# A plain chunk moved to the auxiliary PSUM banks, a later norm product and a reordered weight split in a four-FFN decoder trunk

## The chip, the cores and the metric

One core of a Trainium2 chip runs the whole program in one launch. The metric is the device time of that core in microseconds (us); the time of a kernel is the median of its runs. The engines are named as in the profile: PE (matmul), DVE (vector), ACT (scalar), POOL (GpSimd), and SP, which issues the weight loads.

## What is computed

A decoder trunk over 512 tokens of width 1024, in float32. It has four SwiGLU FFNs (width 2816), with a pooling mixer between the first two and a latent attention between the last two:

```python
def rmsnorm(x, g):
    y = xf * lax.rsqrt(jnp.mean(xf * xf, axis=-1, keepdims=True) + RMS_EPS)
    return (y * g.astype(jnp.float32)).astype(x.dtype)

def swiglu(u, wg, wu, wd):
    return (jax.nn.silu(u @ wg) * (u @ wu)) @ wd
...
    for l in range(DEPTH):
        h = h + 0.5 * swiglu(rmsnorm(h, ffn_pre_norm[l]), ffn_pre_wg[l], ffn_pre_wu[l], ffn_pre_wd[l])
...
        h = h + 0.5 * swiglu(rmsnorm(h, ffn_post_norm[l]), ffn_post_wg[l], ffn_post_wu[l], ffn_post_wd[l])
```

## The kernel before, in words

Activations lie transposed: eight channels of 128 features by 512 tokens (`h[c]`). Float32 operands are split into a rounded high part and a low remainder, and each product takes three matmuls (`mm3`, L116 to L118). A weight tile of 128x1024 is loaded by SP into `wraw`, rounded by ACT (`whi`) and subtracted by DVE (`wlo`); this pair is the split (`load_w` L145, L146; `split_into` L188, L189).

The norm of an FFN is applied late. The matmuls run on `gain*h`, and the per-token factor `r` is multiplied in afterwards. `on_all` (L290) turns `r` into a tile `rb` of 128x512: DVE writes two diagonal tiles (L294, L303), PE multiplies them by ones (L301, L305, "the norm product" here), and ACT copies the result out of PSUM (L307).

PSUM has two pools here. `mm_tile()` hands out six banks in turn, `aux_tile()` two banks in turn. A bank handed out again may be written only when the readers of its last tile are done.

An FFN (`ffn`, L448) makes 22 chunks of 128 hidden features.

- Chunks 0 to 3 are plain: for each of the eight channels a gate and an up product of 512 columns. Chunks 0 and 1 run together in four mm banks, chunk 2 in two more (`m` = 0 gate, 1 up, L570 to L578), chunk 3 in two more (L586 to L589). The norm product is called inside chunk 2. `gated` (L527) then makes the hidden values: DVE multiplies the gate by `rb` (L530), ACT takes the silu (L516), DVE multiplies by `rb` again (L517) and by the up product (L533, which is the last reader of the up bank), and ACT and DVE split the result into `mh`, `ml` (L523, L524).
- Chunks 4 to 21 are the groups (L597). Gate and up weights and two halves of the tokens form 2x2 blocks, and Winograd's seven products take the place of eight. Each product P1 to P7 is 12 matmuls of 256 columns. A group accumulates in three mm tiles, x, y1 and y2. P1, P6, P7 and P4 add to x one after the other, and between them ACT copies x out (`copy_of`, L462: `c1` after P1, `c16` after P6, `c167` after P7). P6 has to wait for the copy `c1`, P7 for the copy `c16`. The operands `t3` of P7 are made by `prepare_t3` in place of half of four `gh` tiles.
- The group's weights come from `group_weights` (L191): two loads, then four splits and four POOL adds (L201). The last split (L213, L214) needs the last add.
- Between the products stand the down products (`down`, L539), 512 columns wide, in aux banks, each output channel `d` in a bank of its own. In group 4 the order on PE is P1, P2, early (d = 0 with chunks 0 and 1, then d = 1 with chunks 0 and 1), P6, P5, middle (d = 0 and 1 with chunk 2), P7. Group 5 goes on with P1, P2 and early (chunk 3).

PE's order is that of the code (`manual_schedule`). On DVE, ACT, POOL and SP a scheduler at build time sets the order; `queued_behind(steps)` tells it that what follows may not be issued ahead of the steps named. In the third FFN `rb` comes from the shared key/value stage ahead of it, so it has no norm product inside chunk 2.

Of the kernel before, what the change touches and what calls it, by code (L numbers as in the profile page):

```python
# [19 lines left out]
ND = D // P  # L20
# [22 lines left out]
def down_steps(g):  # L43


    i, base = g % PART, g - g % PART - PART
    most, end, whole = range(base, base + PART - 1), [base + PART - 1], range(base, base + PART)
    if i == 0 and base == 0:
        return ([(d, most[:2], True, False) for d in range(2)], [(d, most[2:], False, False) for d in range(2)], [])
    if i == 0:  # L50
        return [], [], [(d, most, True, False) for d in range(2)]
    early = [(d, end, False, True) for d in range(2)] if i == 1 else []
    return early, [], [(d, whole, True, True) for d in (2 * i, 2 * i + 1)]
# [15 lines left out]
def trunk_kernel(  # L69
# [23 lines left out]
    nc = tc.nc  # L93
# [11 lines left out]
    def f(ap):  # L105
        return ap.bitcast(F32)

    def mm_tile():
        return psum.tile([P, T], F32, tag="mm", name="mm")

    def aux_tile():
        return psaux.tile([P, T], F32, tag="aux", name="aux")

    def mm3(out, w, x, start, stop, **kw):

        nc.tensor.matmul(out, w[0], x[0], start=start, stop=False, **kw)  # L116
        nc.tensor.matmul(out, w[0], x[1], start=False, stop=False, **kw)  # L117
        nc.tensor.matmul(out, w[1], x[0], start=False, stop=stop, **kw)  # L118
# [61 lines left out]
    def split_w(raw, pool, tag):  # L180
        n = raw.shape[-1]
        hi = pool.tile([P, n], F32R, tag=f"{tag}hi", name=f"{tag}hi")
        lo = pool.tile([P, n], F32R, tag=f"{tag}lo", name=f"{tag}lo")
        return hi, lo

    def split_into(tiles, raw, s):
        hi, lo = tiles
        nc.scalar.copy(hi[:, s], raw[:, s])  # L188
        nc.vector.tensor_tensor(out=lo[:, s], in0=raw[:, s], in1=f(hi[:, s]), op=ALU.subtract)  # L189

    def group_weights(idx, g, wb):  # L191

        ra, rb = (wraw_sb.tile([P, UNIT], F32, tag="wraw", name="wraw") for _ in range(2))
        nc.sync.dma_start(ra, wgu[idx, g - 2, 0])
        nc.sync.dma_start(rb, wgu[idx, g - 2, 1])
        q0, q1, whole = slice(0, 512), slice(512, UNIT), slice(0, UNIT)

        def add(out, x, y):  # L200
            nc.gpsimd.tensor_tensor(out=out, in0=x, in1=y, op=ALU.add)  # L201

        a = split_w(ra, wsplit_sb, "w")
        split_into(a, ra, whole)
        a22 = split_w(rb[:, q0], room.wf, "f")
        split_into(a22, rb[:, q0], q0)
        add(rb[:, q0], rb[:, q0], rb[:, q1])
        add(rb[:, q1], rb[:, q1], ra[:, q0])
        s13 = split_w(rb, wsplit_sb, "w")
        split_into(s13, rb, whole)  # L210
        add(ra[:, q0], rb[:, q0], ra[:, q0])
        add(ra[:, q1], ra[:, q0], ra[:, q1])
        s24 = split_w(ra, wb, "w")  # L213
        split_into(s24, ra, whole)  # L214
        a, a22, s13, s24 = part(a, 8, P), part(a22, 4, P), part(s13, 8, P), part(s24, 8, P)

        def of(w, at):
            return lambda k: [x[:, at + k] for x in w]

        return dict(a11=of(a, 0), a12=of(a, 4), a22=of(a22, 0), s1=of(s13, 0), s3=of(s13, 4), s2=of(s24, 0), s4=of(s24, 4))  # L220
# [4 lines left out]
               before=lambda i, u=u: nc.sync.dma_start(h[2 * u + i], xT[:, 2 * u + i]))  # L225
# [156 lines left out]
    def part(w, *shape):  # L382

        names = "abcd"[:len(shape)]
        spec = f"p ({' '.join(names)}) -> p {' '.join(names)}"
        return [x.rearrange(spec, **dict(zip(names, shape))) for x in w]

    def queued_behind(steps):

        stack = ExitStack()  # L390
        for step in steps:
            stack.enter_context(tc.issue_after(step))
        return stack
# [54 lines left out]
    def ffn(idx, norm, on_h, first=None, last=None):  # L448
        with tc.tile_pool(name="mid", bufs=1) as midp, tc.tile_pool(name="wb", bufs=2) as wb, \
                tc.manual_schedule(engines={mybir.EngineType.PE}):  # L450
            weights, acc, act, mids = {}, {}, {}, {}

            def product(g, to, w, x, start=True):
                if start:
# [4 lines left out]

            def copy_of(g, name):  # L460
                t = act[g][name] = room.act.tile([P, HT], F32, tag=name, name=name)
                nc.scalar.copy(t, acc[g]["x"])  # L462
                return t

            def p1(g):
                product(g, "x", "a11", "b11")
                copy_of(g, "c1")

            def p2(g):
                product(g, "y2", "a12", "b21")  # L470
                y = acc[g]["y2"]
                nc.vector.tensor_tensor(out=y, in0=act[g].pop("c1"), in1=y, op=ALU.add)

            def gate_half(g, i, y):
                if i == 0:
                    act[g]["g"] = room.act.tile([P, T], F32, tag="g", name="gate", bufs=3)
                s = slice(i * HT, (i + 1) * HT)
                nc.vector.tensor_tensor(out=act[g]["g"][:, s], in0=y, in1=rb[:, s], op=ALU.mult)

            def p6(g):  # L480
                product(g, "x", "s2", "t2", start=False)
                copy_of(g, "c16")

            def p5(g):
                product(g, "y1", "s1", "t1")

            def p7(g):
                product(g, "x", "s3", "t3", start=False)
                copy_of(g, "c167")

            def up_half(g):

                t = act[g]["c167"]
                nc.vector.tensor_tensor(out=t, in0=t, in1=acc[g]["y1"], op=ALU.add)

            def p4(g):

                product(g, "x", "a22", "t4", start=False)
# [28 lines left out]
            def gated(g, gate, up):  # L527

                t = room.act.tile([P, T], F32, tag="g", name="gate", bufs=3)
                nc.vector.tensor_tensor(out=t, in0=gate, in1=rb, op=ALU.mult)  # L530
                silu(t)
                m = room.act.tile([P, T], F32, tag="m", name="m", bufs=3)
                nc.vector.scalar_tensor_tensor(out=m, in0=up, scalar=-1.0, in1=t, op0=ALU.mult, op1=ALU.mult)  # L533
                split_mid(g, m)

            units, o_of = {}, {}
            whole = slice(0, T)
# [19 lines left out]
            ps = [mm_tile() for _ in range(4)]  # L557
# [12 lines left out]
            for m in range(2):  # L570
                o = mm_tile()
                for c in range(ND):
                    mm3(o, [x[:, (c + 4 * m) % ND] for x in ws[m]], norm.gh[c], c == 0, c == ND - 1)
                    if m == 1 and c == 0:
                        rb = norm.spread(r, steps)
                        for j in range(2):
                            gated(j, ps[2 * j], ps[2 * j + 1])
                ps.append(o)  # L578
# [4 lines left out]

            with queued_behind(steps):
                weights[N_FIRST] = group_weights(idx, N_FIRST, wb)
            ps = [mm_tile() for _ in range(2)]  # L586
            for c in range(ND):
                for m in range(2):
                    mm3(ps[m], [x[:, (c + 4 * m) % ND] for x in ws[m]], norm.gh[c], c == 0, c == ND - 1)  # L589
# [6 lines left out]
            before = None  # L596
            for g in range(N_FIRST, NF):  # L597
                early, middle, late = down_steps(g)
                if g > N_FIRST:
                    weights[g] = group_weights(idx, g, wb)  # L600
                acc[g], act[g] = {}, {}
                p1(g)
                p2(g)
                gate_half(g, 0, acc[g].pop("y2"))
                for step in early:
                    down(*step, tile_of=aux_tile)
                if before is not None:
                    p4(before)
                p6(g)
                p5(g)  # L610
                for step in middle:
                    down(*step, tile_of=aux_tile)
                if g == NF - 1:
                    p7(g)
                    up_half(g)
                    p3(before)
                    p4(g)
                    p3(g)
                else:
                    if before is not None:  # L620
                        p3(before)
                    p7(g)
                    up_half(g)
                before = g
                for step in late:
                    down(*step, tile_of=aux_tile)
# [15 lines left out]
    nc.sync.dma_start(rope_sb, rope)  # L642
    nxt = Norm(G_MIX)
    ffn(0, norm, nxt.add, first=first_w)

    norm, nxt = nxt, Norm(G_POST)
# [60 lines left out]
    norm, nxt = nxt, Norm(G_PRE + ND)  # L707
    Quarters(nxt, inline=False)
    ffn(1, norm, nxt.add)


# [64 lines left out]
    with tc.tile_pool(name="att", bufs=2) as ap_, tc.tile_pool(name="att1", bufs=1) as a1:  # L776
# [190 lines left out]
        with tc.manual_schedule(engines={engines.PE}):  # L967
            ps = {0: weights(0, qk, nope_first=True)}
# [173 lines left out]
```

## Time and profile before

| | us |
|---|---|
| median of two runs | 1725.56 |
| the two runs | 1724.69, 1726.42 |
| the profiled execution, its own time | 1728.71 |
| its span, first to last instruction | 1726.9 |
| PE busy in the span | 1706.3 (99%) |
| DVE busy | 1302.8 (75%) |
| ACT busy | 850.9 (49%) |
| POOL busy | 570.0 (33%) |

A busy PE is not a PE at full speed: at half clock it is busy too. The mean granted clock of the execution is 0.995 of full speed.

### The profile page before, as it was taken

To read this page: it belongs to the slowest core of one execution; us is meant where nothing else is said; L and a number is where in the kernel's file an instruction comes from. 1 tells how busy PE (TensorE), PEld (TensorE's weight loads), DVE (VectorE), ACT (ScalarE), POOL (GpSimd) and SP (SyncE) were. 2 spreads that over 40 slices of the span, in tenths; PEclk is the share of its full clock that TensorE was granted. 3 is DMA by queue.
4 is the path that set the end of the run, shared out by engine and by line. 5 is a ranking of instruction groups with operands and counts; after the bars stand their busy time and mean duration, and the time that the engine had idled before them with its cause. 6 is when DMAs were issued, how large, how long until landed. Compare 5 with 4: busy or idle time off the path is not lost. (4 is left out here: it accounts for less than half of the span.)

```text
span 1726.9 us, 27436 instructions
## 1 busy us (share of the span) xinstructions
PE 1706.3 (99%) x10816; PEld 1543.4 (89%) x10816; DVE 1302.8 (75%) x2086; ACT 850.9 (49%) x1391; POOL 570.0 (33%) x388
## 2 busy tenths in 40 slices
PE   8999999999999999999999999999999999999998
PEld 6899999998899999888999999888888889999997
DVE  8877777789777777897777777787765787777775
ACT  6544444464444444454444444586655544444443
POOL 2433344133333344113334432422221234334421
PEclk9999999999999999999999999999999999999999
DMA  6233333322333322332333333332231232333331
GB/s 208 86 99 110 110 91 95 121 87 62 110 99 110 109 91 95 106 95 86 111 111 92 94 108 104 94 90 56 61 86 62 72 100 86 111 110 98 95 102 50
DMA packets 49585, 166.77 MB, mean 97 GB/s; under 512 B 6320, under 2 KB 6320, under 8 KB 49456
## 3 DMA queue, kind: packets, MB, share of 16 engines
q1 hardware_dynamic: 49312, 164.98, 31.1%
q8 instruction: 85, 1.39, 0.3%
q14 instruction: 44, 0.36, 0.1%
q10 hardware_dynamic: 144, 0.04, 0.0%
HBM read 158.44 MB, written 2.10 MB: 93 GB/s over the span
## 5 line engine op out<-in xcount | busy, mean ns | idle before, releaser
L201 POOL TENSOR_TENSOR wraw<-wraw 128x512 f32<-128x512 f32 x288 | 438.9, 1525 | 749.2 <-DVE flo L189 703.5
L116 PE MATMUL mm<-gh_hi,whi 128*128 128x256 f32 (+1 forms) x1424 | 435.2, 306 | 6.9 <-ACT c L462 6.9
L118 PE MATMUL mm<-gh_hi,wlo 128*128 128x256 f32 (+1 forms) x1424 | 435.1, 306 | 1.1 <-DVE wlo L146 1.1
L117 PE MATMUL mm<-gh_lo,whi 128*128 128x256 f32 (+1 forms) x1424 | 434.7, 305 | 0.5 <-DVE gh_lo L328 0.5
L188 ACT CAST whi<-wraw 128x1024 fp32r<-128x1024 f32 x216 | 226.9, 1053 | 207.7 <-POOL wraw L201 184.4
L116 PEld LDWEIGHTS mm<-gh_hi,whi 128*128 128x128 f32 x1424 | 274.6, 193 | 21.6 <-ACT c L462 8.6
L117 PEld LDWEIGHTS mm<-gh_lo,whi 128*128 128x128 f32 x1424 | 274.5, 193 | 14.3 <-DVE gh_lo L328 0.9
L118 PEld LDWEIGHTS mm<-gh_hi,wlo 128*128 128x128 f32 x1424 | 274.4, 193 | 13.4 <-DVE wlo L146 2.7
L189 DVE TENSOR_TENSOR wlo<-wraw,whi 128x1024 fp32r<-128x1024 f32 x216 | 271.3, 1257 | 3.1 <-ACT whi L188 3.0
L116 PE MATMUL aux<-mh,whi 128*128 128x512 f32 x576 | 225.3, 391 | 0.0
L117 PE MATMUL aux<-ml,whi 128*128 128x512 f32 x576 | 225.2, 391 | 0.0
L118 PE MATMUL aux<-mh,wlo 128*128 128x512 f32 x576 | 224.1, 389 | 0.0
L146 DVE TENSOR_TENSOR wlo<-wraw,whi 128x1024 fp32r<-128x1024 f32 (+1 forms) x158 | 184.8, 1170 | 31.0 <-ACT whi L145 30.6
L145 ACT CAST whi<-wraw 128x1024 fp32r<-128x1024 f32 (+2 forms) x188 | 162.3, 878 | 86.4 <-PE mm L117 46.7
L504 DVE TENSOR_TENSOR mm<-c,mm 128x256 f32<-128x256 f32 x72 | 30.9, 429 | 197.9 <-PE mm L118 197.9
L116 PE MATMUL mm<-t_hi,whi 128*128 128x256 f32 (+1 forms) x592 | 169.5, 286 | 0.6 <-ACT c L462 0.6
L118 PE MATMUL mm<-t_hi,wlo 128*128 128x256 f32 (+1 forms) x592 | 169.3, 286 | 0.0
L117 PE MATMUL mm<-t_lo,whi 128*128 128x256 f32 (+1 forms) x592 | 169.2, 286 | 0.0
L345 POOL TENSOR_TENSOR sq_acc<-sq_acc,sq 128x512 f32<-128x512 f32 (+1 forms) x47 | 72.5, 1543 | 203.1 <-ACT sq L341 193.4
L517 DVE TENSOR_TENSOR gate<-gate,rb 128x512 f32<-128x512 f32 x88 | 133.6, 1523 | 2.8 <-ACT gate L516 2.8
L462 ACT COPY c<-mm 128x256 f32<-128x256 f32 x216 | 79.8, 370 | 103.9 <-PE mm L118 103.9
L118 PEld LDWEIGHTS aux<-mh,wlo 128*128 128x128 f32 x576 | 108.2, 188 | 23.2
(209 smaller groups left out, 3328.2 us busy)
## 6 DMA issues: line engine op xcount, KB each, us to landing
wraw<-in_wgu SPq DMA_DIRECT2D x160, 512.0 KB, 3.7
wraw<-in_wd SPq DMA_DIRECT2D x88, 512.0 KB, 3.6
wraw<-in_wo SPq DMA_DIRECT2D x16, 512.0 KB, 3.8
wraw<-in_wfirst SPq DMA_DIRECT2D x12, 512.0 KB, 3.6
wraw<-in_wheads SPq DMA_DIRECT2D x8, 512.0 KB, 3.5
h<-in_xT SPq DMA_DIRECT2D x8, 256.0 KB, 5.4
wraw<-in_wfirst SPq DMA_DIRECT2D x8, 256.0 KB, 5.3
qr<-yh SPq DMA_DIRECT2D x32, 64.0 KB, 2.1
```

The costliest lines, as they stand in the source:

```text
L116: nc.tensor.matmul(out, w[0], x[0], start=start, stop=False, **kw)
L117: nc.tensor.matmul(out, w[0], x[1], start=False, stop=False, **kw)
L118: nc.tensor.matmul(out, w[1], x[0], start=False, stop=stop, **kw)
L145: nc.scalar.copy(hi[:, s], raw[:, s]).ins,
L146: lo_engines[i % len(lo_engines)].tensor_tensor(out=lo[:, s], in0=raw[:, s], in1=f(hi[:, s]), op=ALU.subtract).ins]
L188: nc.scalar.copy(hi[:, s], raw[:, s])
L189: nc.vector.tensor_tensor(out=lo[:, s], in0=raw[:, s], in1=f(hi[:, s]), op=ALU.subtract)
L201: nc.gpsimd.tensor_tensor(out=out, in0=x, in1=y, op=ALU.add)
L345: nc.gpsimd.tensor_tensor(out=self.acc[:, ts], in0=self.acc[:, ts], in1=self.sq[:, ts], op=ALU.add)
L462: nc.scalar.copy(t, acc[g]["x"])
L504: nc.vector.tensor_tensor(out=y, in0=act[g]["c16"], in1=y, op=ALU.add)
L517: nc.vector.tensor_tensor(out=gate, in0=gate, in1=rb, op=ALU.mult)
```

## The change

Three edits, all in `ffn` and the functions it calls.

1. Chunk 3's gate and up products go to the two aux banks in place of two mm banks.
2. The call that makes `rb` (the norm product and what follows it) stands in chunk 2 behind channel 4 in place of channel 0, so the two matmuls come four channels (12 matmuls) later.
3. From group 5 on, the group's last split is queued behind the copy `c16` of the group before.

```diff
-    def group_weights(idx, g, wb):
+    def group_weights(idx, g, wb, last_behind=()):
...
         s24 = split_w(ra, wb, "w")
-        split_into(s24, ra, whole)
+        with queued_behind(last_behind):
+            split_into(s24, ra, whole)
...
             def copy_of(g, name):
                 t = act[g][name] = room.act.tile([P, HT], F32, tag=name, name=name)
-                nc.scalar.copy(t, acc[g]["x"])
-                return t
+                copied[g, name] = nc.scalar.copy(t, acc[g]["x"]).ins
...
                     mm3(o, [x[:, (c + 4 * m) % ND] for x in ws[m]], norm.gh[c], c == 0, c == ND - 1)
-                    if m == 1 and c == 0:
+                    if m == 1 and c == ND // 2:
                         rb = norm.spread(r, steps)
...
-            ps = [mm_tile() for _ in range(2)]
+
+            ps = [aux_tile() for _ in range(2)]
...
                 if g > N_FIRST:
-                    weights[g] = group_weights(idx, g, wb)
+                    weights[g] = group_weights(idx, g, wb, [copied[before, "c16"]])
```

The lines of the changed kernel are one to three further down. Three places show what moves; all are taken from the first FFN, and the numbers behind the names are those of the buffers.

PE in group 4, at the end of P2 (`mm_688` is y2) and the early down products: `aux_704` is d = 0 and `aux_711` is d = 1. A name in brackets is the engine whose semaphore the matmul waits for. Before:

```order
L117 MATMUL mm_688<-gh7_lo_259,whi_573 128x256
L118 MATMUL mm_688<-gh7_hi_258,wlo_574 128x256
L116 MATMUL aux_704<-mh0_506,whi_564 128x512 [waits PE_49,Activation_49]
L117 MATMUL aux_704<-ml0_507,whi_564 128x512 [waits DVE_49]
L118 MATMUL aux_704<-mh0_506,wlo_565 128x512
L116 MATMUL aux_704<-mh1_516,whi_564 128x512 [waits Activation_49]
L117 MATMUL aux_704<-ml1_517,whi_564 128x512 [waits DVE_49]
L118 MATMUL aux_704<-mh1_516,wlo_565 128x512
L116 MATMUL aux_711<-mh0_506,whi_564 128x512
L117 MATMUL aux_711<-ml0_507,whi_564 128x512
```

The same place on PE in the changed kernel:

```order
L117 MATMUL mm_688<-gh7_lo_259,whi_573 128x256
L118 MATMUL mm_688<-gh7_hi_258,wlo_574 128x256
L116 MATMUL aux_704<-mh0_518,whi_564 128x512 [waits DVE_49,Activation_49]
L117 MATMUL aux_704<-ml0_519,whi_564 128x512
L118 MATMUL aux_704<-mh0_518,wlo_565 128x512
L116 MATMUL aux_704<-mh1_528,whi_564 128x512 [waits Activation_49]
L117 MATMUL aux_704<-ml1_529,whi_564 128x512
L118 MATMUL aux_704<-mh1_528,wlo_565 128x512
L116 MATMUL aux_711<-mh0_518,whi_564 128x512 [waits DVE_49]
L117 MATMUL aux_711<-ml0_519,whi_564 128x512
```

The order of the matmuls is the same, but the first one of d = 0 and the first one of d = 1 now wait for DVE. The two aux tiles handed out last were chunk 3's gate (`aux_593`) and up (`aux_594`), so d = 0 takes the bank of the gate and d = 1 that of the up product.

DVE around those two readers: `gate_663` is chunk 3's gate, `m_667` its hidden values, `wlo_781` a split of group 5's weights. Before:

```order
L189 TENSOR_TENSOR wlo_590<-wraw_569,whi_589 128x1024
L437 TENSOR_TENSOR gh2_lo_221<-b12_629,gh2_hi_220 128x256
L437 TENSOR_TENSOR gh3_lo_228<-b12_634,gh3_hi_227 128x256
L530 TENSOR_TENSOR gate_663<-mm_593,rb_498 128x512
L189 TENSOR_TENSOR wlo_584<-wraw_570,whi_583 128x1024
L189 TENSOR_TENSOR wlo_771<-wraw_766,whi_770 128x1024
L517 TENSOR_TENSOR gate_663<-gate_663,rb_498 128x512
L472 TENSOR_TENSOR mm_688<-c1_686,mm_688 128x256
L533 SCALAR_TENSOR_TENSOR m_667<-mm_594,gate_663 128x512
L189 TENSOR_TENSOR wlo_781<-wraw_767,whi_780 128x1024
```

The same place on DVE in the changed kernel:

```order
L531 TENSOR_TENSOR gate_663<-aux_593,rb_510 128x512
L189 TENSOR_TENSOR wlo_590<-wraw_569,whi_589 128x1024
L439 TENSOR_TENSOR gh2_lo_221<-b12_629,gh2_hi_220 128x256
L439 TENSOR_TENSOR gh3_lo_228<-b12_634,gh3_hi_227 128x256
L189 TENSOR_TENSOR wlo_584<-wraw_570,whi_583 128x1024
L189 TENSOR_TENSOR wlo_771<-wraw_766,whi_770 128x1024
L518 TENSOR_TENSOR gate_663<-gate_663,rb_510 128x512
L473 TENSOR_TENSOR mm_688<-c1_686,mm_688 128x256
L189 TENSOR_TENSOR wlo_781<-wraw_767,whi_780 128x1024
L534 SCALAR_TENSOR_TENSOR m_667<-aux_594,gate_663 128x512
```

The reader of the gate bank moved ahead of one weight split and two small operations, and the reader of the up bank moved behind one more weight split (`wlo_781`). In the first, second and fourth FFN the order changes in this way; in the third only the names of the banks change on DVE. No instruction changes its place on POOL or SP.

ACT in the same group: `c16_730` is the copy behind P6, `whi_786` the rounding of group 5's last split. Before:

```order
L462 COPY c1_686<-mm_673 128x256
L188 CAST whi_780<-wraw_767 128x1024
L523 CAST mh3_669<-m_667 128x512
L188 CAST whi_786<-wraw_766 128x1024
L462 COPY c16_730<-mm_673 128x256
L145 CAST whi_908<-wraw_907 128x1024
```

The same place on ACT in the changed kernel:

```order
L464 COPY c1_686<-mm_673 128x256
L188 CAST whi_780<-wraw_767 128x1024
L524 CAST mh3_669<-m_667 128x512
L464 COPY c16_730<-mm_673 128x256
L188 CAST whi_786<-wraw_766 128x1024
L145 CAST whi_908<-wraw_907 128x1024
```

The cast and the copy change places, here and at the same point of the other three FFNs; no other group's order changes.

## Rows read from the trace of the kernel before

**Rows 1.** Page, part 1: busy time, share of the span, instructions of each engine.

```profile
PE 1706.3 (99%) x10816; PEld 1543.4 (89%) x10816; DVE 1302.8 (75%) x2086; ACT 850.9 (49%) x1391; POOL 570.0 (33%) x388
```

**Rows 2.** Waits of PE: line, releaser, us in total, times, longest us.

```profile
PE mm L116 <- ACT c L462: 7.5, 5, 2.1
```

**Rows 3.** Timeline of PE and ACT, second FFN, group 4 (start us, us, instruction).

```profile
441.10 0.58 PE L116 MATMUL mm<-gh_hi,whi 128*128 128x256 f32 x1 [2.10 <-ACT c L462]
447.00 0.40 PE L116 MATMUL aux<-mh,whi 128*128 128x512 f32 x1
...
439.73 1.04 ACT L188 CAST whi<-wraw 128x1024 fp32r<-128x1024 f32 x1 [1.82 <-POOL wraw L201]
```

**Rows 4.** Window behind that wait: us, busy of each engine, granted clock, DMA.

```profile
441.00:444.40 3.40, 3.30 (x15) 3.31 (x16) 1.03 (x1) 0.55 (x2) 0.00 (x0) 0.51 0.51 143
```

**Rows 5.** Timeline of PE and DVE, first FFN, from chunk 2 to group 5.

```profile
39.94 0.47 PE L301 MATMUL aux<-diag,ones_r 128*128 128x512 f32 x1 [1.56 <-DVE diag L294]
69.26 0.39 PE L116 MATMUL mm<-gh_hi,whi 128*128 128x256 f32 x1 [0.49 <-ACT c L462]
73.68 0.40 PE L116 MATMUL aux<-mh,whi 128*128 128x512 f32 x1
...
42.25 1.89 DVE L530 TENSOR_TENSOR gate<-mm,rb 128x512 f32<-128x512 f32 x3
64.71 0.68 DVE L533 SCALAR_TENSOR_TENSOR m<-mm,gate 128x512 f32<-128x512 f32 x1
```

**Rows 6.** Timeline of PE, DVE and POOL, second FFN, from chunk 2 to group 4.

```profile
412.17 0.39 PE L301 MATMUL aux<-diag,ones_r 128*128 128x512 f32 x1
412.95 0.50 PE L305 MATMUL aux<-diag,ones_r 128*128 128x512 f32 x1 [0.39 <-DVE diag L303]
428.95 0.28 PE L116 MATMUL mm<-gh_hi,whi 128*128 128x256 f32 x1
...
414.10 1.89 DVE L530 TENSOR_TENSOR gate<-mm,rb 128x512 f32<-128x512 f32 x3
418.34 2.98 DVE L517 TENSOR_TENSOR gate<-gate,rb 128x512 f32<-128x512 f32 x3
436.57 0.68 DVE L533 SCALAR_TENSOR_TENSOR m<-mm,gate 128x512 f32<-128x512 f32 x1
437.17 1.39 DVE L189 TENSOR_TENSOR wlo<-wraw,whi 128x1024 fp32r<-128x1024 f32 x1
...
416.67 2.90 POOL L201 TENSOR_TENSOR wraw<-wraw 128x512 f32<-128x512 f32 x2 [12.96 <-DVE flo L189]
```

**Rows 7.** Windows: us; PE, PEld, DVE, ACT, POOL busy; granted clock; DMA.

```profile
414.10:436.57 22.47, 22.47 (x120) 19.36 (x119) 22.47 (x29) 13.62 (x23) 9.93 (x7) 1.00 0.19 58
42.25:64.71 22.46, 22.46 (x107) 18.90 (x107) 22.46 (x29) 13.61 (x23) 9.93 (x7) 0.94 0.21 56
1393.67:1416.14 22.47, 22.45 (x119) 19.10 (x118) 22.47 (x30) 14.49 (x24) 9.95 (x7) 1.00 0.20 55
```

**Rows 8.** Timeline of PE and DVE, third FFN, groups 4 and 5.

```profile
796.22 0.39 PE L116 MATMUL aux<-mh,whi 128*128 128x512 f32 x1
798.34 0.39 PE L116 MATMUL mm<-t_hi,whi 128*128 128x256 f32 x1 [0.60 <-ACT c L462]
810.90 0.40 PE L116 MATMUL aux<-mh,whi 128*128 128x512 f32 x1
...
800.48 0.69 DVE L533 SCALAR_TENSOR_TENSOR m<-mm,gate 128x512 f32<-128x512 f32 x1
```

**Rows 9.** Timeline of PE and DVE, fourth FFN, from chunk 2 to group 5.

```profile
1392.33 0.39 PE L305 MATMUL aux<-diag,ones_r 128*128 128x512 f32 x1
1426.58 0.40 PE L116 MATMUL aux<-mh,whi 128*128 128x512 f32 x1
...
1393.67 1.88 DVE L530 TENSOR_TENSOR gate<-mm,rb 128x512 f32<-128x512 f32 x3
1416.14 0.68 DVE L533 SCALAR_TENSOR_TENSOR m<-mm,gate 128x512 f32<-128x512 f32 x1
```

More of the change, by code (lines that the diff above doesn't have):

```diff
@@ L450, in ffn @@
                 tc.manual_schedule(engines={mybir.EngineType.PE}):
-            weights, acc, act, mids = {}, {}, {}, {}
+            weights, acc, act, mids, copied = {}, {}, {}, {}, {}
             def product(g, to, w, x, start=True):
```

## The prediction

> **What bounds the kernel now.** I read the busy times first. PE is busy for 99% of the span [rows 1], so the time is PE's own work, and only what PE waits for, or loses to a lower clock, can be won or lost. Then the waits of PE: the largest by far is P6 or P7 waiting for ACT's copy of x, 7.5 us in five times [rows 2]. The timeline shows it in the second FFN. P7 of group 4 waits 2.10 us because the copy `c16` stands on ACT behind a weight cast (439.73), and that cast waits for POOL's adds, with which P7 has nothing to do [rows 3]. Four of the five waits are before P7 of group 4, one in each FFN; the fifth is 0.60 us before P6 in the third [rows 8].
>
> The wait costs twice. In the 3.4 us behind it the granted clock is 0.51 [rows 4], that is the lower of the two levels, 1.2 GHz. P7, P1 and P2 are 36 matmuls of 256 columns. In the first FFN, where the wait is 0.49 us, they take 73.68 - 69.26 = 4.42 us [rows 5], so 0.123 us each; in the second 447.00 - 441.10 = 5.90 us [rows 3]. The slow stretch costs 1.48 us.
>
> Last I read DVE between the arrival of the norm factor `rb` and the hidden values m(3) of chunk 3. In the first, second and fourth FFN DVE is busy for all of the 22.46 to 22.47 us from the first L530 to m(3) (L533) [rows 7]. It is the full engine there, though nothing of PE waits for m(3) at once: chunk 3's mm banks are next used in group 5.
>
> **The change part by part.** A matmul of 512 columns takes (428.95 - 412.95) / 70 = 0.229 us [rows 6]: behind the norm product there are 21 matmuls of chunk 2 and 48 of chunk 3.
>
> *Weight split behind `c16`.* The four waits before P7 go: 7.5 less the 0.60 in the third FFN, so 6.9 us, and the slow stretch behind three of them, 4.4 us. The split is late for nobody, since P6 of group 5 is the first to read it. Alone this edit is worth about 11 us.
>
> *Norm product four channels later.* It stands 12 x 0.229 = 2.75 us later. In the first FFN PE waits 1.56 us for the diagonal tile [rows 5], in the second 0.39 us for its remainder [rows 6]; both are covered by the 2.75 us. In the first the granted clock of 0.94 over the next 22.46 us [rows 7] is a further 1.35 us. The gain is about 3.3 us. The price is `rb`: L530 begins 414.10 - 412.95 = 1.15 us after the second matmul (L305) [rows 6]. Second FFN: L305 comes to 412.17 + 2.75 + 0.23 = 415.15, L530 to 416.30, 2.20 us later than before. Fourth: L305 1392.33 + 2.75, L530 at 1396.23 in place of 1393.67 [rows 9], 2.56 us later. First: PE was free at 39.94 - 1.56 = 38.38, so L305 comes to 41.36 and L530 to 42.51 in place of 42.25, 0.26 us later. DVE is full, so m(3) moves by as much. In the third FFN `rb` is made elsewhere and nothing moves.
>
> *Chunk 3 in the aux banks.* PE did not wait for the mm banks of chunk 3, so nothing is won. What is added is the wait that the order of PE shows: d = 0 of group 4 needs L530's read of the gate, d = 1 needs m(3)'s read of the up product. Behind d = 1 on PE stand P6, P5, the middle products, P7 and everything after. On DVE m(3) now has one more weight split ahead of it, in the three FFNs where the order changed: 1.39 us [rows 6]. The trace shows no price for this wait; it follows from when m(3) is done.
>
> PE's arrival, second FFN: P1 began at 428.95 [rows 6] and loses the 0.55 us that L305 had waited and restarted; P1 and P2 are 24 x 0.123 = 2.95, d = 0 is 6 x 0.229 = 1.37, so PE stands at d = 1 at 432.7. m(3) ends at 436.57 + 0.68 + 2.20 + 1.39 = 440.84. The wait is about 8 us, ahead of the P7 wait that the other edit removes.
>
> *The sum.* I compare the start of group 5's early products. From the end E of m(3) there are d = 1 (1.37), P6 and P5 (2.95), the middle products (1.37), P7, P1, P2 (4.43), and one slow stretch behind a pause this long, taken at the 1.48 us above: E + 11.60.
>
> - First FFN: E = 64.71 + 0.68 + 0.26 + 1.39 = 67.04, early at 78.64, before 73.68: +4.96.
> - Second: E = 440.84, 452.44, before 447.00: +5.44.
> - Third [rows 8]: E = 800.48 + 0.69 = 801.17, 812.77, before 810.90: +1.87. PE would stand at d = 1 from 796.22.
> - Fourth [rows 9]: E = 1416.14 + 0.68 + 2.56 + 1.39 = 1420.77, 1432.37, before 1426.58: +5.79.
>
> Together +18.1 us. From group 5 on PE has no wait to give this back. The profiled execution takes 1728.71 us and would take 1746.8; it lies 3.15 us above the median of the runs, so for the median I predict 1725.56 + 18.1 = 1743.7 us.
>
> *Unknown prices.* The slow stretch: none (PE may be back at full clock before d = 1) to two of them, -5.9 to +5.9 us over four FFNs. The DVE stretch: three L517 beside POOL's adds (416.67, 2.90 us) took 2.98 us, three L530 of the same size 1.89 [rows 6], so an add that meets such an operation costs DVE 1.09 us, and POOL has seven adds, 9.93 us, in the stretch [rows 7]. The order of DVE changes there, so up to two fewer or one more may meet: -2.2 to +1.1 us in three FFNs, -6.6 to +3.3. I take both as measured.
>
> The Trainium skill (SBUF - State Buffer, section Who interferes with whom) says that a DVE instruction with two SBUF inputs and a GpSimd instruction that reads SBUF shut each other out for a whole instruction, while one with a single SBUF input does not contend. The trace agrees: L517 with two SBUF inputs is the slow one, L530, whose gate lies in PSUM, is not. By this rule the stretch would fall to its uncontended length if all adds met operations with a PSUM input, and d = 1 would come earlier; that is the second rival.
>
> **The rivals.**
>
> 1. *The banks come free in time (the other side).* If m(3) were done when PE gets to d = 1, only the gains would stay: 11.3 + 3.3, about 14.6 us, so 1711. For it: these two banks are read by two DVE operations only, and gate's reader moved forward. Against it: DVE is full before m(3), and m(3) would have to be 8 us sooner. The point from which it decides: at 18.1 / 4 = 4.5 us sooner in each FFN the change is even; below that it is slower than before.
> 2. *The wait is there, but short.* DVE meets two adds fewer in three FFNs and the clock is back early: 1743.7 - 6.6 - 5.9 = 1731.2. For it: the order before m(3) is new. Against: POOL's six adds up to the first split still have to run inside the stretch.
> 3. *The pause costs the clock twice.* A pause of 8 us against 2.10 us may leave PE at 1.2 GHz for a second stretch: 1743.7 + 5.9 = 1749.6, and with one more meeting in three FFNs 1752.9. For it: the pause is longer than any in these rows. Against: in rows 4 the slow part ends after one stretch of steady work.
> 4. *The edits do nothing.* The scheduler might keep cast and copy as they were; but the order of ACT shows them exchanged, so the P7 wait goes or is replaced.
>
> **How the numbers follow.** The forecast 0.78, rival 1 0.04, rival 2 0.09, rival 3 0.08, rival 4 0.01. Low and high are the ends of rivals 2 and 3, 1731 and 1752. Two per cent, 34.5 us, is about what a measurement of this kernel can tell from no change; every case lies inside it (rival 1 is 0.8% faster, rival 3 1.6% slower). I leave 0.01 for faster and 0.04 for slower, in case the long pauses cost more than two stretches.
>
> **What would show it.** Right: in the waits of PE a new row, an aux matmul (L116) waiting for DVE's m (the changed kernel's L534), four times, up to 8 us, about 5 in the third FFN and about 8 in the others; no wait of P7 for a copy; no wait at the norm product in the first and second FFN; a granted clock near half in the first microseconds behind each d = 1; DVE full from `rb` to m(3), some 24 us. Wrong: no wait at d = 1, or one much under 5 us in the first, second and fourth FFN, or a wait of P7 that stays.

## The result, and the profile after

The changed kernel takes 1751.2 us (median of two runs, 1749.26 and 1753.13) against 1725.56 before: ratio 1.0151, 95% interval 1.0126 to 1.0175. It is slower by 25.6 us, or 1.5%: less than the 2% that the prediction took as the least that can be told from no change, but well outside the interval. A second measurement, later (e5 below), gave 1751.55 (four runs, ratio 1.0145, 1.013 to 1.016). The prediction was 1743.7, range 1731 to 1752, so the measured time lies just inside its upper end.

The profiled execution took 1749.26 us with a span of 1747.5, so 20.55 us more than the profiled one of before (1728.71). PE's waits, which answer to [rows 2] (line, releaser, us in total, times, longest):

```profile
PE aux L116 <- DVE m L534: 14.8, 4, 4.9
PE aux L116 <- DVE gate L531: 9.1, 3, 3.4
PE aux L116 <- ACT whi L188: 3.4, 1, 3.4
PE mm L118 <- DVE wlo L146: 1.2, 2, 0.8
```

The wait of P7 for the copy is gone from the list, and so are the waits of the norm product. In their place stand down products (`aux`): four times for m, the hidden values of chunk 3, and four times for the reader of the gate. In the third row the view names ACT, but that place in the second FFN is the same d = 0 as in the three others, and the gate's reader (L531) ended 0.1 us before PE went on, so I count it to the gate. This is the timeline of PE and DVE in the second FFN, to be laid beside [rows 3] and [rows 6]; all of it begins 6.84 us later than before, because the first FFN took that much longer:

```profile
441.54 0.47 PE L116 MATMUL aux<-mh,whi 128*128 128x512 f32 x1 [3.40 <-ACT whi L188]
448.97 0.79 PE L116 MATMUL aux<-mh,whi 128*128 128x512 f32 x1 [4.90 <-DVE m L534]
...
423.00 1.89 DVE L531 TENSOR_TENSOR gate<-mm,rb 128x512 f32<-128x512 f32 x3 [2.14 <-ACT rb L309]
440.75 0.68 DVE L531 TENSOR_TENSOR gate<-aux,rb 128x512 f32<-128x512 f32 x1
446.36 1.95 DVE L189 TENSOR_TENSOR wlo<-wraw,whi 128x1024 fp32r<-128x1024 f32 x1
448.24 0.68 DVE L534 SCALAR_TENSOR_TENSOR m<-aux,gate 128x512 f32<-128x512 f32 x1
```

PE stands before d = 0 until the gate is read (441.43), does the products of two chunks, and stands before d = 1 until m(3) has read the up product (448.92). DVE has nothing to spare in between: the windows from L531 to the end of m(3) in the first, second and fourth FFN (columns as in [rows 7]) show it busy for all but 0.07 of 26.1 us and for all of 25.9 us, PE for some 18 us.

```profile
42.00:68.10 26.10, 18.19 (x85) 14.78 (x83) 26.03 (x33) 13.23 (x24) 12.49 (x8) 0.84 0.21 61
423.00:448.90 25.90, 17.67 (x85) 14.33 (x83) 25.90 (x32) 13.08 (x23) 12.44 (x8) 0.87 0.15 53
1409.80:1435.70 25.90, 17.92 (x84) 14.55 (x83) 25.90 (x32) 14.42 (x24) 12.48 (x8) 0.93 0.14 47
...
449.00:452.20 3.20, 3.20 (x9) 2.62 (x10) 0.93 (x2) 0.57 (x1) 0.44 (x1) 0.50 0.56 164
```

The last row is the stretch behind d = 1 in the second FFN: granted clock 0.50, the lower level of the two.

Where the time went shows at the start of group 5's early products, the point that the prediction used. Its rows, in the four FFNs:

```profile
80.52 0.40 PE L116 MATMUL aux<-mh,whi 128*128 128x512 f32 x1
460.48 0.40 PE L116 MATMUL aux<-mh,whi 128*128 128x512 f32 x1
824.55 0.40 PE L116 MATMUL aux<-mh,whi 128*128 128x512 f32 x1
1447.12 0.40 PE L116 MATMUL aux<-mh,whi 128*128 128x512 f32 x1
```

Less the rows of before (73.68, 447.00, 810.90, 1426.58) this is 6.84, 13.48, 13.65 and 20.54 us of delay, so each FFN added:

| FFN | forecast | measured |
|---|---|---|
| first | +4.96 | +6.84 |
| second | +5.44 | +6.64 |
| third | +1.87 | +0.17 |
| fourth | +5.79 | +6.89 |
| sum | +18.1 | +20.5 |

The sum is the difference of the two profiled executions to 0.1 us, so on balance nothing is lost or won elsewhere.

### The profile page after: what moved, and what is told of

The parts are those of the page before. It is cut to its first block, busy times and chain, and to the rows that moved or that the text cites. A ratio compares the mean times of both kernels' runs of the same rounds, so it can differ in the third digit from the quotient of the medians.

```text
span 1747.5 us, 27434 instructions
## 1 busy us (share of the span) xinstructions
PE 1709.7 (98%) x10816; PEld 1545.4 (88%) x10816; DVE 1304.7 (75%) x2086; ACT 849.5 (49%) x1391; POOL 568.7 (33%) x388
## 3 DMA queue, kind: packets, MB, share of 16 engines
q8 instruction: 85, 1.39, 0.3%
## 4 chain that ended last, share of the span: by engine, by line
PE 87%; DVE 9%; ACT 1%; issue 1%; DMA 1%; SPq 0%; DVEq 0%; ACTq 0%
PE mm L116 20%; PE mm L117 20%; PE mm L118 20%; PE aux L116 8%; PE aux L117 8%; PE aux L118 7%; DVE wlo L189 1%; DVE wlo L146 1%; DVE gate L518 1%; PE mm L892 1%; PE aux L929 1%; DVE gh_lo L439 1%; DVE gh_lo L330 1%; PE mm L904 1%; PE mm L894 1%
## 5 line engine op out<-in xcount | busy, mean ns | idle before, releaser
L118 PE MATMUL mm<-gh_hi,wlo 128*128 128x256 f32 (+1 forms) x1360 | 407.2, 299 | 1.2 <-DVE wlo L146 1.2
L117 PE MATMUL mm<-gh_lo,whi 128*128 128x256 f32 (+1 forms) x1360 | 407.1, 299 | 0.5 <-DVE gh_lo L330 0.5
L116 PE MATMUL mm<-gh_hi,whi 128*128 128x256 f32 (+1 forms) x1360 | 407.2, 299 | 0.0
L117 PEld LDWEIGHTS mm<-gh_lo,whi 128*128 128x128 f32 x1360 | 259.9, 191 | 11.7 <-DVE gh_lo L330 0.9
L116 PEld LDWEIGHTS mm<-gh_hi,whi 128*128 128x128 f32 x1360 | 259.9, 191 | 10.7
L118 PEld LDWEIGHTS mm<-gh_hi,wlo 128*128 128x128 f32 x1360 | 259.9, 191 | 10.1 <-DVE wlo L146 1.9
L116 PE MATMUL aux<-mh,whi 128*128 128x512 f32 x576 | 229.4, 398 | 27.3 <-DVE m L534 14.8
L116 PEld LDWEIGHTS aux<-mh,whi 128*128 128x128 f32 x576 | 110.0, 191 | 51.1 <-DVE m L534 17.7
```

## The experiments

### One edit or two of the three

**Edit 3 alone (e1)**: the changed kernel with the other two edits taken back.

```diff
-                    if m == 1 and c == ND // 2:
+                    if m == 1 and c == 0:
...
-            ps = [aux_tile() for _ in range(2)]
+            ps = [mm_tile() for _ in range(2)]
```

> Edit 3 alone: the last split of weights behind the copy c16; norm product and chunk 3 as before. My theory (the gain of edit 3 is real, and lost in the whole change only behind the wait for the aux banks): the four waits of P7 (0.49 + 2.10 + 2.14 + 2.14 us) and the slow clock behind three of them (1.48 us each) go, 11.3 us, so 1714 us. Rival (edit 3 is worth nothing, the copy is late for other reasons): 1725 us, and P7 waits for the copy as before.

Measured: 1716.67 us, ratio to before 0.995 (0.9935 to 0.9965); again, as e11, 1715.75, ratio 0.9935 (0.9923 to 0.9947). The theory holds, at 8.9 to 11.0 us of the 11.3 expected by medians; between the profiled executions (1716.66 and 1728.71) it is 12.05 us. On ACT in the second FFN the copy now follows `mh`, ahead of the cast that waits for POOL:

```profile
437.00 0.62 ACT L524 CAST mh<-m 128x512 fp32r<-128x512 f32 x1 [1.96 <-DVE m L534]
437.52 0.37 ACT L464 COPY c<-mm 128x256 f32<-128x256 f32 x1
439.45 1.05 ACT L188 CAST whi<-wraw 128x1024 fp32r<-128x1024 f32 x1 [1.56 <-POOL wraw L202]
```

and of PE's waits for copies one is left, before P6 in the third FFN:

```profile
PE mm L116 <- ACT c L464: 0.4, 1, 0.4
```

**Edit 1 alone (e2)**: chunk 3 in the aux banks, the rest as before.

```diff
-                    if m == 1 and c == ND // 2:
+                    if m == 1 and c == 0:
...
-                    weights[g] = group_weights(idx, g, wb, [copied[before, "c16"]])
+                    weights[g] = group_weights(idx, g, wb)
```

> Edit 1 alone: chunk 3 in the two aux banks; norm product and last split as before. My theory: d = 1 of group 4 waits for m(3) in all four FFNs, with m(3) when it was before (its end at 65.4, 437.3, 801.2 and 1416.8 us of the trace of before); the wait of P7 for the copy disappears behind it. From the end of m(3) to the early products of group 5 the changed kernel took 10.1 to 12.4 us, so +1.5 to +4 us in the first FFN and 0 to +2.5 in each of the others: 1728 to 1735 us, middle 1732. Rival (the later norm product is what costs, the aux banks alone are harmless): 1724 to 1727 us, with no wait of an aux matmul for m(3).

Measured: 1737.73 us, ratio 1.0072 (1.0057 to 1.0087). The aux banks are not harmless; they cost 12 us by themselves, 3 us more than the top of what was expected. In the profiled execution (1735.39) it is only 6.7 us, and there the four FFNs add 3.89, 1.94, 0.48 and 0.36 us up to the early products of group 5, each inside the expectation. So the miss lies in the step from one profiled execution to the median. The waits are the expected ones, and P7's is hidden:

```profile
PE aux L116 <- DVE m L534: 8.4, 4, 2.1
PE aux L116 <- DVE gate L531: 3.0, 2, 1.9
PE aux L116 <- ACT whi L188: 1.6, 1, 1.6
PE aux L303 <- DVE diag L296: 1.5, 1, 1.5
```

**Edits 2 and 3 (e3)** without edit 1.

```diff
-            ps = [aux_tile() for _ in range(2)]
+            ps = [mm_tile() for _ in range(2)]
```

> Edits 2 and 3 without edit 1: chunk 3 stays in the mm banks. My theory: without the aux banks no down product waits for m(3), so the kernel is faster than before. But DVE is full from rb to m(3) and rb is 2.2 us later in the second and fourth FFN, so P6 now waits for the copy c1 (in the changed kernel it ended 2.2 us after P6 could have started), and part of the gain is given back: 1714 to 1721 us. Rival (the later norm product by itself makes the kernel slower, whatever the banks): 1728 us or more. Second rival (the later norm product is free): 1711 us, the sum of both gains.

Measured: 1720.08 us, ratio 0.9971 (0.996 to 0.9981). Faster than before, 3.4 us slower than edit 3 alone. So the later norm product by itself doesn't make the loss, and it isn't free (the second rival had 1711): `rb` and what hangs on it are late for PE. Its price stands in the second FFN in two waits for `ml` and one of P6 for the copy `c1`:

```profile
430.70 0.50 PE L117 MATMUL aux<-ml,whi 128*128 128x512 f32 x1 [0.51 <-DVE ml L525]
432.10 0.50 PE L117 MATMUL aux<-ml,whi 128*128 128x512 f32 x1 [0.43 <-DVE ml L525]
435.00 0.39 PE L116 MATMUL mm<-t_hi,whi 128*128 128x256 f32 x1 [0.79 <-ACT c L464]
```

**Edits 1 and 3 (e4)** without edit 2.

```diff
-                    if m == 1 and c == ND // 2:
+                    if m == 1 and c == 0:
```

> Edits 1 and 3 without edit 2: norm product where it was. My theory: the wait for m(3) hides what edit 3 gives, so this kernel takes the same time as edit 1 alone, within 2 us (1728 to 1735), some 15 to 20 us less than the whole change, whose m(3) comes 2.2 to 2.6 us later from rb and 1.4 to 1.9 us later from the extra split ahead of it. Rival (the gains add up): 11 us faster than edit 1 alone, about 1721 us.

Measured: 1737.16 us, ratio 1.0067 (1.0052 to 1.0082), that of edit 1 alone within 0.6 us, as expected, though 2 us above the range named, and 14 us less than the whole change, a little less than the 15 to 20 expected. What edit 3 saves lies behind the wait for m(3) and is worth nothing there.

Step by step, by medians: edit 3 takes 8.9 us off, edit 2 on top of it gives back 3.4, edit 1 on top of both costs 31.5 (1751.55 - 1720.08). These are not prices of the edits as such: edit 1 alone costs 12.2 (1737.73 - 1725.53). With the bank's wait in place edit 3 gains nothing, and edit 2 costs 14 us in place of 3.4, because it makes m(3) late.

### Which of the two banks

The changed kernel again (e5), as the measure for the three below and the one after them.

> The changed kernel once more, as the measure for the three runs beside it. 1749 to 1753 us, as in its first two runs.

Measured: 1751.55 us.

Two kernels (e6 and e7) that differ from each other in one thing only: which product of chunk 3 lies in an aux bank. Since the banks are handed out in turn, d = 0 takes a bank that has long been free in both, and d = 1 the bank of chunk 3.

```diff
-            ps = [aux_tile() for _ in range(2)]
+            ps = [aux_tile(), mm_tile()]
```

> The changed kernel with only the gate of chunk 3 in an aux bank, the up product in an mm bank. d = 1 of group 4 then waits for the read of the gate (L531) alone, and d = 0 for nothing of chunk 3; edits 2 and 3 as in the change. My theory (the late reader of the up bank, m(3), is what costs): the read of the gate ends some 2 us after PE could start d = 1, and P6 waits for the copy c1 until about then anyway, so nearly the time of edits 2 and 3 without the aux banks, 1720 us, at most 8 us more for slow clock: 1720 to 1728. Rival (any wait for an aux bank at this place costs about the same): 1740 us or more.

```diff
-            ps = [aux_tile() for _ in range(2)]
+            ps = [mm_tile(), aux_tile()]
```

> The changed kernel with only the up product of chunk 3 in an aux bank, the gate in an mm bank. d = 1 of group 4 waits for m(3), d = 0 for nothing of chunk 3. My theory: m(3) is done when it was in the whole change, so the time is that of the whole change, 1745 to 1753 us, with one pause of some 7 to 9 us before d = 1 in place of two. Rival (two pauses, one for each bank, are what costs): half of the loss, about 1735 us.

Measured: with the gate in an aux bank 1720.25 us, ratio 0.9965 (0.9952 to 0.9978), the time of the kernel with no aux bank; with the up product there 1751.14, ratio 1.0145 (1.0128 to 1.0162), the time of the whole change. The aux bank of the gate costs nothing and that of the up product everything. The waits of the two say the same, first those of the kernel with the gate in an aux bank:

```profile
PE aux L117 <- DVE ml L525: 3.6, 9, 0.5
PE aux L116 <- DVE gate L531: 1.4, 3, 0.5
```

and of the kernel with the up product there:

```profile
PE aux L116 <- DVE m L534: 28.5, 4, 8.0
PE aux L117 <- DVE ml L525: 2.8, 6, 0.5
```

Two pauses of 3.4 and 4.9 us became one of 8.0, at no difference in time: d = 1 waits for the same m(3), and the pause before d = 0 in the change was only a part of that wait.

### The size of the wait: the clock, and the split ahead of m(3)

**Work in the pauses (e8).** Matmuls on zeros, whose result nothing reads, before d = 0 and d = 1 of group 4, in three FFNs.

```diff
+                if g == N_FIRST and idx != 2:
+                    acc[g]["y1"] = mm_tile()[:, :HT]
+                for n, step in zip((26, 36), early):
+                    for _ in range(n if g == N_FIRST and idx != 2 else 0):
+                        nc.tensor.matmul(acc[g]["y1"], blank[:, :P], blank, start=True, stop=True)
-                for step in early:
                     down(*step, tile_of=aux_tile)
```

> The changed kernel with matmuls on zeros, whose result nothing reads, put before d = 0 (26 of them) and d = 1 (36) of group 4 in the first, second and fourth FFN, 256 columns each, to keep PE at work in the pauses. My theory (the slow clock behind the pauses is part of the loss; from d = 1 to the early products of group 5 the changed kernel took 12.4, 11.5 and 11.4 us in these FFNs where full clock would take 10.1): 3 to 5 us less than the changed kernel, with no slow stretch there. Rival (the wait alone is the loss): the same time, or more where the fill is longer than the pause.

Measured: 1747.37 us, ratio to before 1.0119 (1.0104 to 1.0135), 4.2 us less than the changed kernel. So part of the loss is the clock and not the wait: m(3) came no sooner, since from the first L531 to d = 1 it took 25.98, 25.97 and 25.98 us in the three FFNs, in the change 25.98, 25.97 and 25.96. The trace shows it clean in the fourth FFN alone, where the pause before d = 1 shrank to 1.83 us, the stretches on either side stayed at full clock, and the way from d = 1 to the early products took 10.09 us in place of 11.40:

```profile
1435.18 0.50 PE L116 MATMUL aux<-mh,whi 128*128 128x512 f32 x1 [1.83 <-DVE m L534]
...
1432.00:1437.00 5.00, 3.17 (x22) 2.51 (x20) 4.15 (x6) 0.62 (x1) 3.58 (x2) 1.00 0.51 171
1437.00:1442.00 5.00, 5.00 (x38) 4.74 (x38) 1.23 (x1) 1.32 (x2) 0.00 (x0) 1.00 0.14 37
```

In the second FFN the fill ended 1.86 us before d = 1 could start, and the clock fell all the same:

```profile
448.05 0.69 PE L116 MATMUL aux<-mh,whi 128*128 128x512 f32 x1 [1.86 <-DVE m L534]
...
447.90:450.40 2.50, 2.35 (x6) 1.88 (x7) 1.12 (x3) 0.62 (x1) 0.62 (x1) 0.56 0.62 205
```

From d = 1 to group 5's early products this FFN took 453.96 + 5.70 - 448.05 = 11.61 us, as in the change (11.51), where 5.70 us is the way from the middle products on at full clock. There nothing was won (in the first FFN 0.8 us, 11.57 for 12.39), so 4.2 us is not the whole price of the clock.

**m(3) ahead of the split (e9).** The split that the scheduler had put ahead of m(3) is queued behind it (`made3` is m(3)'s DVE instruction, which `gated` now returns).

```diff
-        split_into(s13, rb, whole)
+        with queued_behind(s13_behind):
+            split_into(s13, rb, whole)
...
-                    weights[g] = group_weights(idx, g, wb, [copied[before, "c16"]])
+                    weights[g] = group_weights(idx, g, wb, [copied[before, "c16"]], [made3] if g == N_FIRST + 1 else ())
```

> The changed kernel with one thing more: the split that had come ahead of m(3) on DVE in the first, second and fourth FFN (wlo_781, second split of group 5) is queued behind m(3). My theory: m(3) ends sooner by that operation, which took 1.39 us before the change and 1.9 us in the changed kernel, and PE's pause before d = 1 is shorter by as much: 4 to 6 us less than the changed kernel, 1744 to 1748 us. Rival (DVE waits for something else there, such as ACT or POOL, and m(3) stays): 1751 us.

Measured: 1744.68 us, ratio to before 1.0104 (1.009 to 1.0118), 6.9 us less than the changed kernel in e5. The two ran on different chips, but the ratios (1.0104 and 1.0145) say the same, 7 us. In the second FFN, DVE and PE:

```profile
420.43 1.89 DVE L532 TENSOR_TENSOR gate<-mm,rb 128x512 f32<-128x512 f32 x3 [2.15 <-ACT rb L310]
443.79 0.68 DVE L535 SCALAR_TENSOR_TENSOR m<-aux,gate 128x512 f32<-128x512 f32 x1
444.39 1.35 DVE L189 TENSOR_TENSOR wlo<-wraw,whi 128x1024 fp32r<-128x1024 f32 x1
...
444.52 0.80 PE L116 MATMUL aux<-mh,whi 128*128 128x512 f32 x1 [3.35 <-DVE m L535]
```

From L531 (here L532) to the end of m(3) it is 444.47 - 420.43 = 24.04 us, in the change 448.92 - 423.00 = 25.92: the split's 1.88 us. Three times that is 5.6 of the 6.9 us. PE doesn't get all of it in every FFN: in the second, d = 1 to the early products took 12.50 us for 11.51 (444.52 to 457.02), as the low clock lasted longer.

### A version that beats both

Edit 3 with the norm product later only where PE had waited for it (e10).

```diff
-                    if m == 1 and c == 0:
+                    if m == 1 and c == {0: ND // 2, 1: 1}.get(idx, 0):
```

> Edit 3, and edit 2 only where PE waited for the norm product: four channels later in the first FFN, one in the second, as before in the others; chunk 3 in the mm banks. My theory: the first FFN took 1.6 us less in the run with edits 2 and 3 than in the run with edit 3 alone, and the other two lost 1.9 and 2.3 us there from the later factor, which this kernel keeps; so 1.6 to 2 us less than edit 3 alone, about 1714.8 us, the fastest of all. Rival (the gain at the norm product is given back at P6 in the first FFN too): the time of edit 3 alone, 1716.7 us.

Measured: 1715.68 us, ratio 0.9935 (0.9922 to 0.9949), beside edit 3 alone on the same chip (e11):

> Edit 3 alone again, on the same chip as the kernel beside it: 1716 to 1717 us.

Measured: 1715.75 us, a little under what was expected. No difference to e10, so the theory missed. In the trace of e10 P6 and P7 of the second FFN waited 1.5 us for copies that they don't wait for with edit 3 alone, so one channel was too much there. The last run (e12) moved the product in the first FFN only:

```diff
-                    if m == 1 and c == 0:
+                    if m == 1 and c == (ND // 2 if idx == 0 else 0):
```

> Edit 3, and edit 2 in the first FFN alone (four channels later), nothing moved in the second. My theory: in the run that also moved the second FFN's norm product by one channel, the first FFN was 2.2 us shorter than with edit 3 alone and the second 1.4 us longer (P6 and P7 waited 1.5 us for copies); without that loss 1 to 2.5 us less than edit 3 alone: 1713.5 to 1715 us. Rival (what the first FFN gains is lost further down): 1715.7 to 1716.7 us, as edit 3 alone.

Measured: 1714.53 us, ratio 0.9936 (0.9924 to 0.9949). By its median the fastest of all and inside the expectation, but it ran at another time than e10 and e11, and its ratio to before is theirs (0.9935). What beats both kernels for sure is edit 3; whether the first FFN's norm product adds to it stays open at about 1 us. The profiled executions speak for it: the early products of group 5 in the first FFN begin at 71.70 us, with edit 3 alone at 73.46 (e1) and 73.30 (e11).

## Why the prediction was right, and where its sizes were off

**Direction and place.** The cause stood in the order of PE and DVE: the early products take over the banks of chunk 3, and d = 1 waits for m(3) at the end of a stretch in which DVE is full. The trace shows the wait four times, and e6 against e7 shows that the reader of the up bank alone makes the loss. The first rival (the banks come free in time) fell by about 8 us: with one pause instead of two (e7) PE stood 8.0 us. Its time was wrong too: e3 has both gains and no wait for a bank, and took 1720.08 us, not 1711. The mechanism held, the size less so: 25.6 us were measured for 18.1, and that the median stayed inside the range by 0.8 us is luck in part.

**The three edits.** That edit 3 is worth some 9 to 11 us alone and that this gain goes under in the wait is shown by e1 and e11 (8.9 and 11.0 us) and by e4 against e2 (0.6 us). Edit 2's price through a late `rb` was in the sum: e4 has no late `rb` and no extra split, and takes 14 us less than the change. E3 shows that without the aux banks the late `rb` costs 3.4 us more than it wins, which the prediction had not worked out, as m(3) covered it. The prediction lists the extra split under the aux banks; the runs show that edit 2 brings it. With edits 2 and 3 and no aux bank (e3) it stands ahead of m(3), with edit 1 alone (e2) behind it. Second FFN, first e3, then e2:

```profile
438.18 1.98 DVE L189 TENSOR_TENSOR wlo<-wraw,whi 128x1024 fp32r<-128x1024 f32 x1
440.09 0.68 DVE L534 SCALAR_TENSOR_TENSOR m<-mm,gate 128x512 f32<-128x512 f32 x1
...
440.51 0.68 DVE L534 SCALAR_TENSOR_TENSOR m<-aux,gate 128x512 f32<-128x512 f32 x1
441.12 1.35 DVE L189 TENSOR_TENSOR wlo<-wraw,whi 128x1024 fp32r<-128x1024 f32 x1
```

**The pause before d = 0** was named in the change part, but PE's arrival at d = 1 was worked out as if it did not occur. It changes the look of the waits, not the sum, since d = 1 waits for m(3) either way. So of the signs named beforehand the sizes are off: before d = 1 PE stood 4.49, 4.90 and 4.56 us in place of about 8, and 0.87 in place of about 5 in the third FFN. DVE was full for 26 us in place of some 24. The other signs came, save one: the clock near half behind d = 1 was seen in three FFNs and not in the third.

**Mis-sized, first: the split ahead of m(3).** The prediction took the 1.39 us of before. The operation took 1.95 us, and from L531 to the end of m(3) it was 25.92 us, where 22.47 + 0.68 + 1.39 = 24.54 was forecast. Half a microsecond is the split itself (1.88 us to the next start, e9), the rest is other DVE operations: two `gh_lo` took 2.35 us for 1.84 before, one `wlo` 2.31 for 1.93 (a `flo` took 1.1 us longer and the `ml` 1.1 us less). That is about the upper bound of the prediction's "one more meeting" in each FFN. It is not that these operations came to lie beside POOL's adds: the split, the `wlo` and the longer `gh_lo` lay beside adds before, too. But splits of the same form take 1.21 us where no add runs, and the split ahead of m(3) lies beside two adds. The changed kernel, and the adds of before beside the split at 437.17 [rows 6]:

```profile
441.35 1.21 DVE L189 TENSOR_TENSOR wlo<-wraw,whi 128x1024 fp32r<-128x1024 f32 x1
445.64 3.80 POOL L202 TENSOR_TENSOR wraw<-wraw 128x512 f32<-128x512 f32 x2 [8.88 <-issue]
...
435.80 3.90 POOL L201 TENSOR_TENSOR wraw<-wraw 128x512 f32<-128x512 f32 x2 [7.30 <-DVE wlo L189]
```

So how an operation falls against the single adds seems to set its length: begun 1.37 us into these adds the split took 1.39 us, begun 0.72 us into them 1.95. m(3), with an input in PSUM, took 0.68 us beside the adds both times. The Trainium skill (SBUF — State Buffer, section Who interferes with whom) says that a DVE instruction with two SBUF inputs contends with a GpSimd instruction that reads SBUF, and one with at most one SBUF input, outside the 2-port modes, does not. The rows agree with it. L530 in [rows 6], which the prediction called in for the second half, doesn't bear on it: it ended at 415.99, before the first add at 416.67. No run here took POOL's adds away, so the contention is argued and not shown. In all, d = 1 began 1.09, 1.29 and 1.30 us later than the forecast E in the three FFNs, 3.7 us together, and 0.16 us sooner in the third.

**Mis-sized, second: the clock.** Four slow stretches of 1.48 us behind d = 1 were taken. From d = 1 to the early products full clock takes 10.12 us; it took 12.39, 11.51, 10.06 and 11.40 us (d = 1 began at 68.13, 448.97, 814.49 and 1435.72). So the low clock cost 2.3, 1.4, nothing and 1.3 us. In the third FFN the slow stretch lay ahead of d = 1, over the products of d = 0, where it cost nothing because PE had to wait for m(3) anyway:

```profile
810.69:814.00 3.31, 2.93 (x6) 1.82 (x6) 3.31 (x5) 1.82 (x3) 0.96 (x1) 0.50 0.69 215
814.49:818.85 4.36, 4.36 (x31) 4.10 (x31) 2.92 (x3) 1.79 (x3) 2.30 (x2) 1.00 0.52 166
```

That is why it came out at +0.17 for +1.87. Together the four are 1.0 us less than the 5.9 taken, and with the above the profiled execution is explained: 18.1 + 3.7 - 0.2 - 1.0 = 20.6, measured 20.5.

**The rest of the median.** The larger part of the miss is not in the FFNs. The prediction worked from one execution of before, 3.15 us above the median of its kernel, and took that distance to stay; the profiled execution of the change lies 1.9 us under its median. So of the 7.5 us between 1743.7 and 1751.2, 5.1 come from this step and 2.4 from the sum. The time of a run goes with its granted clock: of the later runs of the kernel before, the 15 at 0.997 took 1723.8 to 1727.1 us and the five at 0.995, the clock of the profiled one, 1728.1 to 1730.3; the first two of the changed kernel took 1749.3 at 0.990 and 1753.1 at 0.987. So the execution of before that was read had more slow clock in it than most. The profiled execution of e5 shows where runs of the changed kernel differ. Behind d = 1 of the fourth FFN the clock stayed at the lower level for longer, where the first trace shows 0.58 from 1435.70 to 1439.20 and then 1.00; and in the third FFN the slow stretch lay behind d = 1, and from there to the early products it took 11.59 us for 10.06:

```profile
1436.20:1440.00 3.80, 3.19 (x9) 2.62 (x10) 1.57 (x3) 0.62 (x1) 1.08 (x1) 0.50 0.42 138
1440.00:1443.50 3.50, 3.50 (x21) 3.50 (x20) 0.00 (x0) 1.12 (x2) 0.00 (x0) 0.59 0.03 5
...
814.80:818.20 3.40, 3.40 (x14) 3.05 (x13) 2.13 (x3) 0.00 (x0) 1.58 (x1) 0.50 0.51 163
```

The fourth FFN is the third rival (the pause costs the clock twice). How often it comes in other runs no trace shows; the clocks on record fit with it.

## What to carry to other kernels

Before a tile moves to another pool of banks, look up who takes that pool's next tile and when the last reader of this one is done. Here the reader at the end of a full stretch of DVE set the price, and moving only the tile with the early reader may be free, as here with the gate. An edit that removes a wait is worth nothing as long as a longer wait ends behind it, so parts of a change are to be timed one by one: here one of the three alone was faster than before and the three together slower. And before a sum is laid on one profiled execution, look how its time and its clock lie among the other runs.

## What the runs showed that was not expected

A pause under two microseconds had two outcomes in the same execution of e8: behind 1.86 us in the second FFN the granted clock was 0.56, behind 1.83 us in the fourth it was 1.00. So the price of a pause can't be read from its length alone, and a sum over a few pauses is uncertain by a microsecond or so for each: in two executions of the changed kernel the same way from d = 1 took 10.06 and 11.59 us in the third FFN, 11.40 and 12.75 in the fourth.
